# Channel shuffle in place: tiles of 23 KB a partition in place of 24 KB, and a 6 KB tile last

## The chip, the cores and the metric

One core of one Trainium2 chip. Times are device microseconds of one execution; medians of several executions are given. "Span" is the length of the profiled execution as the trace has it, about 1.8 us less than the time of the same execution. A "packet" is what the DMA records list: one row, that is the bytes of one partition of a tile, carried by one of the 16 DMA engines.

## The reference

```python
batch, h, w, c = 16, 64, 64, 256          # float32, groups = 8
x = x.reshape(batch, h, w, groups, c // groups)
x = x.transpose(0, 1, 2, 4, 3)            # channel g*32+j goes to j*8+g
x = x.reshape(batch, h, w, c)
```

67.1 MB come in and 67.1 MB go out; each pixel's 256 floats (1 KB) are permuted in the same way. There is no arithmetic.

## The kernel before

The pixels are cut into tiles of 128 partitions with q pixels (q KB) a partition. A tile is loaded by one DMA on the load queue (issued by SyncE), permuted in pieces of 8 KB a partition by VectorE into PSUM (a second on-chip memory), copied back in place by ScalarE, and stored by one DMA on the store queue (issued by ScalarE). In HBM a partition's q KB are contiguous, and the next partition's follow at once, so "KB between rows" is q as well.

```python
_SIZES = [24] * 20 + [8, 24]
_BUFS = 8
_PIECE = 8
...
    for q in _SIZES:
        buf = pool.tile([P, biggest * c], F32, name="buf")
        nc.sync.dma_start(out=buf[:, : q * c], in_=rows(x_flat, first, q))
        for k in range(0, q, _PIECE):
            piece = buf[:, k * c : (k + _PIECE) * c]
            bounce = psum.tile([P, _PIECE * c], F32, name="bounce")     # two of these
            nc.vector.tensor_copy(out=bounce..., in_=piece...)          # "p (i g j) -> p i j g"
            nc.scalar.copy(out=piece, in_=bounce)
        nc.scalar.dma_start(out=rows(out_flat, first, q), in_=buf[:, : q * c])
        first += P * q
```

## Time and profile before

| | before |
|---|---|
| time, median of the 3 runs that the prediction had | 317.83 us (317.72 to 317.91) |
| span | 315.9 us |
| VectorE, ScalarE busy | 227.9 us, 120.3 us |
| load queue, store queue, share of 16 engines | 49.9%, 49.4% |
| HBM traffic | 134.2 MB, 425 GB/s over the span |

How to read it: the two queue shares are time that packets took, as a share of 16 DMA engines' span, so their sum tells how full the DMA engines are. VectorE at 72% and DMA at 99.3% are averages; which of them sets the end has to be read from stretches and waits.

### The profile page before, as it was taken

The numbers are of one execution on the slowest core, as the hardware profiler recorded it, in microseconds if no ns is written. First come the engines' busy times: TensorE is split into PE (matmuls) and PEld (weight loads), VectorE is DVE, ScalarE is ACT, GpSimd is POOL, SyncE is SP. The second block draws the span as 40 slices with busy tenths as digits, with TensorE's granted clock in tenths as the row PEclk, the third lists the DMA queues.
The fourth block names the chain that finished last, engine by engine and source line by source line (L and its number), as shares of the span: only waits on it lengthen the run. The fifth ranks groups of instructions, "written<-read, shape, count | busy, mean of one in ns | idle before, by whom it ended". The sixth has DMA issues, their size and how long they took to land.

```text
span 315.9 us, 289 instructions
## 1 busy us (share of the span) xinstructions
DVE 227.9 (72%) x64; ACT 120.3 (38%) x65; POOL 0.2 (0%) x4
## 2 busy tenths in 40 slices
DVE  0699999959587685957008986999970299999900
ACT  0354455525252424330015416545500444555420
POOL 0000000000000000000000000000000000000000
DMA  8999999999999999999999999999999999999997
GB/s 296 439 442 380 436 429 433 433 439 433 423 442 433 426 442 426 426 442 426 433 436 427 433 436 436 433 426 437 433 423 448 423 429 444 429 423 433 439 432 302
DMA packets 6338, 134.24 MB, mean 425 GB/s; under 512 B 704, under 2 KB 704, under 8 KB 704
## 3 DMA queue, kind: packets, MB, share of 16 engines
q1 hardware_dynamic: 3168, 67.11, 49.9%
q10 hardware_dynamic: 3168, 67.11, 49.4%
q14 instruction: 2, 0.02, 0.0%
HBM read 67.11 MB, written 67.11 MB: 425 GB/s over the span
## 4 chain that ended last, share of the span: by engine, by line
DVE 54%; another core or an unknown queue 23%; issue 8%; ACT 5%; DMA 3%; DVEq 1%; ACTq 0%
DVE bounce L54 54%; ACT buf L58 5%; DMA buf<-in_x_dram 3%; DVEq L91 1%; ACTq L59 0%; DVEq L54 0%; ACTq L58 0%
## 5 line engine op out<-in xcount | busy, mean ns | idle before, releaser
L54 DVE COPY bounce<-buf 128x2048 f32<-128x2048 f32 x64 | 227.9, 3636 | 72.6 <-ACT buf L58 38.8
L58 ACT COPY buf<-bounce 128x2048 f32<-128x2048 f32 x64 | 119.0, 1866 | 171.1 <-DVE bounce L54 115.3
L58 ACT ACT_TABLE_LOAD x1 | 1.3, 1283 | 11.1 <-DMA buf<-in_x_dram 11.1
L77 POOL MEMSET const-bfloat16-1.0<- 128x1 bf16 x1 | 0.1, 102 | 0.0
L77 POOL MEMSET const-uint8-127<- 128x1 uint8 x1 | 0.1, 101 | 0.0
L77 POOL MEMSET const-float32-0.0<- 128x1 f32 x1 | 0.1, 99 | 0.2 <-issue 0.2
L77 POOL MEMSET const-float32-1.0<- 128x1 f32 x1 | 0.1, 98 | 0.0
## 6 DMA issues: line engine op xcount, KB each, us to landing
buf<-in_x_dram SPq DMA_DIRECT2D x21, 3072.0 KB, 58.4
out_dram<-buf ACTq DMA_DIRECT2D x21, 3072.0 KB, 24.2
buf<-in_x_dram SPq DMA_DIRECT2D x1, 1024.0 KB, 46.0
out_dram<-buf ACTq DMA_DIRECT2D x1, 1024.0 KB, 15.8
```

What stands on the lines that cost most here:

```text
L54: nc.vector.tensor_copy(out=bounce.rearrange("p (i j g) -> p i j g", j=CPG, g=G), in_=piece.rearrange("p (i g j) -> p i j g", g=G, j=CPG),)
L58: nc.scalar.copy(out=piece, in_=bounce)
L77: nc = _bacc.Bacc("TRN2", target_bir_lowering=False, num_devices=1)
L91: with _tile.TileContext(nc) as tc:
```

## The change

Its intent, by its title: rows an odd number of KB apart (kinder to memory), and a small tile last (a shorter tail). Everything else is meant to stay, the eight buffers too.

```diff
-_SIZES = [24] * 20 + [8, 24]
+_SIZES = [23] * 22 + [6]
 _BUFS = 8
+_STORE = 23
 _PIECE = 8
...
-        for k in range(0, q, _PIECE):
-            piece = buf[:, k * c : (k + _PIECE) * c]
...
-        nc.scalar.dma_start(out=rows(out_flat, first, q), in_=buf[:, : q * c])
+        for a in range(0, q, _STORE):
+            b = min(a + _STORE, q)
+            for k in range(a, b, _PIECE):
+                piece = buf[:, k * c : min(k + _PIECE, b) * c]
...                                      # the same two copies, on 8, 8 and 7 KB
+            cols = slice(a * c, b * c)
+            nc.scalar.dma_start(out=rows(out_flat, first, q)[:, cols], in_=buf[:, cols])
```

More of the change, by code (lines that the diff above doesn't have):

```diff
@@ L26 @@
     nc = tc.nc
-    b, h, w, c = x.shape
+    n, h, w, c = x.shape
     G = int(groups)
@@ L30 @@
     assert G * CPG == c
-    assert sum(_SIZES) * P == b * h * w
+    assert sum(_SIZES) * P == n * h * w
     biggest = max(_SIZES)
@@ L50 @@
         nc.sync.dma_start(out=buf[:, : q * c], in_=rows(x_flat, first, q))
-        for k in range(0, q, _PIECE):
-            piece = buf[:, k * c : (k + _PIECE) * c]
-            bounce = psum.tile([P, _PIECE * c], F32, name="bounce")
-            nc.vector.tensor_copy(
-                out=bounce.rearrange("p (i j g) -> p i j g", j=CPG, g=G),
-                in_=piece.rearrange("p (i g j) -> p i j g", g=G, j=CPG),
-            )
-            nc.scalar.copy(out=piece, in_=bounce)
-        nc.scalar.dma_start(out=rows(out_flat, first, q), in_=buf[:, : q * c])
+        for a in range(0, q, _STORE):
+            b = min(a + _STORE, q)
+            for k in range(a, b, _PIECE):
+                piece = buf[:, k * c : min(k + _PIECE, b) * c]
+                bounce = psum.tile([P, _PIECE * c], F32, name="bounce")
+                nc.vector.tensor_copy(
+                    out=bounce[:, : piece.shape[1]].rearrange("p (i j g) -> p i j g", j=CPG, g=G),
+                    in_=piece.rearrange("p (i g j) -> p i j g", g=G, j=CPG),
+                )
+                nc.scalar.copy(out=piece, in_=bounce[:, : piece.shape[1]])
+            cols = slice(a * c, b * c)
+            nc.scalar.dma_start(
+                out=rows(out_flat, first, q)[:, cols], in_=buf[:, cols]
+            )
         first += P * q
```

## The prediction

> **What bounds the kernel now.** I read the page's first two sections first, to see which resource is full, then the DMA queues, then a table of stretches to see where it is not full, then the waits, to see whether the compute engines have room, and last the packet records behind the DMA rows. Busy shares and slices of the page:
>
> ```profile
> span 315.9 us, 289 instructions
> DVE 227.9 (72%) x64; ACT 120.3 (38%) x65; POOL 0.2 (0%) x4
> ...
> DVE  0699999959587685957008986999970299999900
> ...
> DMA  8999999999999999999999999999999999999997
> ...
> q1 hardware_dynamic: 3168, 67.11, 49.9%
> q10 hardware_dynamic: 3168, 67.11, 49.4%
> ```
>
> The reader is to see that VectorE has holes in the middle (whole slices at 0), ScalarE is at 38%, and the DMA row is at 9 in every slice but the first and the last. The load queue (q1) and the store queue (q10) together fill 49.9 + 49.4 = 99.3% of 16 engines' span. The kernel moves 67.11 MB in and 67.11 MB out, so this is a copy with a shuffle hidden inside it. How well is it hidden, and where is the rate lost? The table of stretches (columns: stretch, its length, busy time of each engine with counts, clock, DMA share, GB/s):
>
> ```profile
> 0.00:8.00 8.00, 0.00 (x0) 0.00 (x0) 0.20 (x4) 1.00 0.82 301
> 8.00:24.00 16.00, 12.95 (x4) 6.88 (x4) 0.00 (x0) 1.00 1.01 433
> 24.00:32.00 8.00, 8.00 (x3) 3.73 (x2) 0.00 (x0) 1.00 1.02 399
> 32.00:160.00 128.00, 92.99 (x27) 46.63 (x25) 0.00 (x0) 1.00 1.00 432
> 160.00:286.00 126.00, 99.42 (x28) 53.70 (x29) 0.00 (x0) 1.00 1.01 432
> ...
> 314.00:316.00 2.00, 0.00 (x0) 0.00 (x0) 0.00 (x0) 1.00 0.00 0
> ```
>
> From 8 us to the last 2 us the rate is 432 to 433 GB/s, except for one dent from 24 to 32 us, where the first stores begin beside the loads. The dent costs 8 x (1 - 399/433) = 0.6 us, and the start 8 x (1 - 301/433) = 2.4 us. The waits:
>
> ```profile
> DVE bounce L54 <- ACT buf L58: 38.8, 4, 18.8
> DVE bounce L54 <- DMA buf<-in_x_dram: 33.9, 7, 11.1
> SPq L50 <- DMA out_dram<-buf: 209.9, 14, 22.0
> ```
>
> VectorE waits for data and for ScalarE (which in turn stood 55.7 us waiting for loads), and the load queue's issuer waits 209.9 us for stores to free a buffer. None of these waits costs time, because the table shows the DMA engines full meanwhile: while a load is held back, stores run, and the other way round. So the end is set by bytes over 16 DMA engines. The page's chain of waits, 54% VectorE and 23% unknown queue, is not the bound: it follows one sequence of releases, and the DMA is full under all of it.
>
> The packet records say the same to the nanosecond. A 24576-byte row takes 912 ns in both queues from the 10th to the 90th percentile, and the 8192-byte rows of the one small tile take 309 ns, all 256 of them. Hence (912 - 309) / 16384 = 0.0368 ns a byte (27.2 GB/s an engine) plus 309 - 8192 x 0.0368 = 7.5 ns a row. Each engine moves 8 rows of each tile in each direction.
>
> **What the Trainium skill says.** "DMA: Bandwidth & Descriptors", section "Where 436 GB/s comes from", puts a ceiling of 435.2 GB/s on 16 engines and their ports, shared by all that the core moves. The trace agrees: 16 x 27.2 GB/s is 435, and 432 to 433 with the 7.5 ns a row. The kernel is at that ceiling. Its section "Why small descriptors are slow" has a fixed cost for each packet of about 3 cycles; the trace has 7.5 ns a row, larger, but under 1% of a 24 KB row. Its section "Latency and other measured facts" has HBM row pitches at large powers of two slowing copies (512 KiB and up), cured by a pad of 4 KiB. That is the only ground I find for wanting an odd number of KB between rows. The trace speaks against it here: the pitch is 24 KB, not of that kind, and the rows already move at the ceiling rate. "SBUF — State Buffer", section "SBUF: two separate sides", says that engine accesses and DMA do not contend; in this trace the DMA rate is 432 to 433 GB/s while VectorE is busy and 428 or more when it is not, so different compute piece sizes should not touch it.
>
> **The change part by part.**
>
> The tiles: 22 of 23 KB a partition and one of 6 KB, in place of 21 of 24 KB and one of 8 KB (second to last). Bytes are equal: 22 x 23 + 6 = 21 x 24 + 8 = 512 KB a partition. Row times by the line above: 23552 bytes: 7.5 + 866.8 = 874.3 ns; 6144 bytes: 7.5 + 226.1 = 233.6 ns.
> - Before, each engine: 21 x 8 x 2 = 336 rows x 912 ns = 306.43 us, and 16 x 309 ns = 4.94 us, together 311.38 us, with 44 completion packets of 9 ns (0.40 us) 311.78 us.
> - After, each engine: 22 x 8 x 2 = 352 rows x 874.3 ns = 307.75 us, and 16 x 233.6 ns = 3.74 us, together 311.49 us, with 46 completion packets (0.41 us) 311.90 us.
> - Difference: +0.12 us, on the path.
>
> The copies: each 23 KB tile is worked as 8 + 8 + 7 KB, so there are 22 x 3 + 1 = 67 pieces in place of 64. The order of VectorE and ScalarE is otherwise unchanged; the loop over stores has one round, as 23 is the whole tile. In an unbroken stretch successive ScalarE copies start 3.55 us apart (14.69, 18.24, 21.79 us), that is 0.444 us for each KB, so a 23 KB tile takes about 10.2 us of VectorE. Its two transfers take 2 x 8 x 874.3 ns = 14.0 us. VectorE keeps 27% of room, and the three extra pieces are hidden.
>
> The buffers: still eight, of 23 KB, so 184 KB in flight in place of 192. The store that frees a buffer comes a little earlier for each tile. This only rearranges the waits that cost nothing.
>
> The start: the first store was issued at 23.7 us. With a first load shorter by 128 KB (0.3 us at 433 GB/s) and a last piece shorter by 1 KB (0.44 us) it comes at about 22.9 us. The engines are full of loads then, so nothing is won. The first data moves at 1.74 us in either case.
>
> The end: in before the last data packet ends at 314.56 us and the span 1.3 us later. The last load had landed by 285.7 us; from there on there were (314.56 - 285.7) x 433 GB/s = 12.5 MB of stores to move, four tiles, about two of them already queued. The last store was issued at 302.5 us, so 12.1 us of stores lay before the end, of which its own 3.15 MB are 7.3 us: 4.8 us of older stores still stood in the queue. The final tile's compute chain is therefore already hidden, and a smaller last tile wins nothing there. It can't shorten a tail that is full of bytes.
>
> The sum: 317.83 + 0.12 = 317.95 us. I round to 318.0.
>
> **The rivals.**
>
> 1. The odd pitch helps memory. For it: the diff's wording, and the skill's note on pitch. Against it: the rows have no spread to gain; all of the time that load packets took above 912 ns comes to 1.76 us an engine, about 0.95 of it in the first packets (the ramp) and 0.76 in the dent. If the dent went away entirely, the time would be 318.0 - 0.7 = 317.3 us. It can't reach 2%: even with no dent and no ramp, first data at 1.74 us, 311.9 us of packets, 1.3 us of end and the 1.9 us between span (315.9) and measured time (317.8) give 316.8 us.
>
> 2. A smaller last tile shortens the tail. For it: the usual gain of such a tile where the last store is exposed. Against it: the 4.8 us of older stores that stood before it. It would make nothing of the time; at most it lowers the risk of a gap.
>
> 3. The phases shift so that the engines run dry at the end: after the last load lands, VectorE feeds a tile only each 10.2 us, while a store drains one in 7.0 us; with few stores queued at that moment the queue would empty. For it: the load and store queues swing (VectorE has slices of 0 and slices of 9), and which of the two is long when the loads end is a matter of phase. Against it: stores lag loads from the first 22 us on, in which only loads run (about 9 MB, three tiles), and the lag shrinks only while no load is queued. With 9 MB (21 us) of stores open and at most two tiles (23 + 6 KB, 13 us of VectorE and 2 of ScalarE) uncomputed, there is no gap. If it happened, 1 to 4 us: 319 to 322 us.
>
> 4. A 23 KB row costs more than the line says (some size that is not a multiple of 8 KB split badly by the engine). The trace before has only two sizes, so the line is untested between them. 2% would need 18 ns more a row; both sizes divide by 256 bytes, and I see no reason.
>
> **Range and chances.** The arithmetic leaves +0.1 us; rivals 1 and 2 could take 0.7 to 1.2 us off, rivals 3 and 4 could add 1 to 4. Executions of one kernel agree within about 0.1 us here (317.72 to 317.91). So 318.0 us, with 316.8 to 319.4 for 8 times in 10. Faster by over 2% means under 311.5 us, less than the packets alone take: 1%. Slower by over 2% means over 324.2 us, which needs a gap longer than any I can construct: 2%. Within 2%: 97%.
>
> **What would show it.** Right: packets of about 874 ns for the 23 KB rows in both queues and 234 ns for the 6 KB rows; a DMA row at 9 in all slices but the ends; 432 to 433 GB/s from 32 us to near the end; a span of about 316.0 us; VectorE's busy time within 2% of 227.9 us in 67 pieces, and its holes moved but harmless. Rival 1 would show no dent around 24 to 32 us. Rival 3 would show slices under 9 near the end and VectorE busy up to the last few us. Rival 4 would show packets over 880 ns. The prediction is wrong if the middle stretches hold anything but 432 to 433 GB/s, or if the DMA stands idle between the first load and the last store.

## The result, and the profile after

The changed kernel takes 317.60 us (median of 4, 317.42 to 317.69) beside 317.77 us for the kernel before (317.69 to 317.91, now with a fourth run). The ratio is 0.9993, 95% interval 0.9976 to 1.0011: the same. (A ratio is the mean time of one kernel's fast runs over that of the other's of the same rounds, so it is not quite the ratio of the medians.)

Page of the changed kernel: busy shares, slices and queues.

```profile
span 315.8 us, 300 instructions
DVE 228.1 (72%) x67; ACT 120.9 (38%) x68; POOL 0.2 (0%) x4
...
DMA  8999999999999999999999999999999999999997
...
q1 hardware_dynamic: 3312, 67.11, 49.9%
q10 hardware_dynamic: 3312, 67.11, 49.4%
```

The DMA row and the two shares are those of before to the last digit, with 3312 packets a queue in place of 3168. Its table of stretches, cut at the same times as before (stretch, length, busy time of the engines with counts, clock, DMA share, GB/s):

```profile
8.00:24.00 16.00, 13.11 (x4) 6.67 (x4) 0.00 (x0) 1.00 1.00 430
24.00:32.00 8.00, 8.00 (x4) 4.32 (x3) 0.00 (x0) 1.00 0.99 383
32.00:160.00 128.00, 98.74 (x29) 49.53 (x28) 0.00 (x0) 1.00 1.00 433
160.00:286.00 126.00, 93.09 (x28) 50.89 (x29) 0.00 (x0) 1.00 1.00 432
286.00:303.00 17.00, 15.15 (x5) 9.50 (x6) 0.00 (x0) 1.00 1.00 432
```

The long stretches stay at 432 to 433 GB/s, and the dent at 24 to 32 us is still there (383 GB/s, 399 before; by the packet records the long load packets cost each engine 0.78 us, 0.76 before). The waits moved by a few us and still cost nothing:

```profile
DVE bounce L58 <- DMA buf<-in_x_dram: 36.5, 8, 10.9
DVE bounce L58 <- ACT buf L62: 36.4, 2, 18.5
SPq L52 <- DMA out_dram<-buf: 215.2, 15, 21.8
```

In the packet records the 23 KB rows take 874 ns in both queues from the 10th to the 90th percentile, and the 6 KB rows 234 ns. From the first data packet to the end of the last one it is 312.79 us, and 312.82 us before.

### The profile page after: what moved, and what is told of

It is laid out like the page before. It is cut to its first block, busy times and chain, and to the rows that moved or that the text cites. A ratio compares the mean times of both kernels' runs of the same rounds, so it can differ in the third digit from the quotient of the medians.

```text
span 315.8 us, 300 instructions
## 1 busy us (share of the span) xinstructions
DVE 228.1 (72%) x67; ACT 120.9 (38%) x68; POOL 0.2 (0%) x4
## 3 DMA queue, kind: packets, MB, share of 16 engines
q1 hardware_dynamic: 3312, 67.11, 49.9%
q10 hardware_dynamic: 3312, 67.11, 49.4%
## 4 chain that ended last, share of the span: by engine, by line
DVE 47%; DMA 25%; another core or an unknown queue 16%; issue 4%; ACT 3%; DVEq 1%; ACTq 0%; SPq 0%
DVE bounce L58 47%; DMA buf<-in_x_dram 19%; DMA out_dram<-buf 7%; ACT buf L62 3%; DVEq L98 1%; ACTq L64 0%; DVEq L58 0%; ACTq L62 0%; SPq L52 0%
## 5 line engine op out<-in xcount | busy, mean ns | idle before, releaser
L58 DVE COPY bounce<-buf 128x2048 f32<-128x2048 f32 (+2 forms) x67 | 228.1, 3481 | 73.1 <-DMA buf<-in_x_dram 36.5
L62 ACT COPY buf<-bounce 128x2048 f32<-128x2048 f32 (+2 forms) x67 | 119.6, 1790 | 170.8 <-DVE bounce L58 120.0
## 6 DMA issues: line engine op xcount, KB each, us to landing
out_dram<-buf ACTq DMA_DIRECT2D x1, 768.0 KB, 12.2
```

What stands on the lines that cost most here:

```text
L58: nc.vector.tensor_copy(out=bounce[:, : piece.shape[1]].rearrange("p (i j g) -> p i j g", j=CPG, g=G), in_=piece.rearrange("p (i g j) -> p ...
L62: nc.scalar.copy(out=piece, in_=bounce[:, : piece.shape[1]])
```

## The experiments

All are edits of the changed kernel, which was 317.60 us; each was timed against the kernel before on its own chip (median 317.57 to 317.62 us in all three sets), so a difference to 317.6 us can be read directly.

### 1. No compute at all

```diff
-            for k in range(a, b, _PIECE):
-                ... both copies ...
```

> The changed kernel with the VectorE and ScalarE copies taken out: every tile is loaded and stored unshuffled (a wrong result on purpose). If 16 DMA engines' bytes set the end, as I hold: 317.6 us as for the changed kernel, within 316.5 to 319 (the last store can't start before the last load has landed, which may now leave a small gap at the end), and packets of 874 ns as before. Rival, that part of the compute chain (47% VectorE in the page's chain) lies on the path: at least 6 us less, under 311.6 us. Rival, that compute slows the DMA: packets under 874 ns.

Measured: 317.19 us (317.14 to 317.51), ratio to before 0.9986 (0.9971 to 1.0001). The result is wrong: loads and stores alone. Page and stretches of this kernel (its table has a column for GpSimd only):

```profile
span 315.4 us, 124 instructions
...
8.00:16.00 8.00, 0.00 (x0) 1.00 1.00 389
32.00:160.00 128.00, 0.00 (x0) 1.00 1.00 432
```

What follows: taking away 228 us of VectorE and 120 us of ScalarE work wins at most some 0.4 us, inside the interval of "the same". The compute chain, 47% of the page's chain of the changed kernel, is not on the path, and the packets are 874 ns with or without it, so compute doesn't slow the DMA. The dent came earlier, with the earlier stores (the 8 to 16 us stretch, 389 GB/s).

### 2. An even pitch: 22 KB

```diff
-_SIZES = [23] * 22 + [6]
+_SIZES = [22] * 23 + [6]        # and _STORE = 22
```

> The changed kernel with 23 tiles of 22 KB and the 6 KB tile: an even number of KB between rows. The row model (7.5 ns + 0.0368 ns a byte) gives 22528-byte packets of 836.6 ns and 312.05 us of packets an engine against 311.90: 317.75 us. Rival, that an odd pitch is better for memory: packets longer than 837 ns and more than 318.5 us.

Measured: 317.63 us (317.50 to 317.95), ratio 0.9996 (0.9980 to 1.0013); packets of 836 ns. What follows: odd or even makes no difference that runs with a scatter of 0.2% can show.

### 3. A power-of-two pitch: 16 KB

```diff
-_SIZES = [23] * 22 + [6]
+_SIZES = [16] * 32              # _STORE = 16
-_BUFS = 8
+_BUFS = 11
```

> 32 tiles of 16 KB, a power of two between rows[...], with 11 buffers so that 176 KB stay in flight. The row model gives 16384-byte packets of 610.5 ns, 512 rows and 64 completions an engine: 313.16 us of packets against 311.90, so 318.9 us. Rival, that power-of-two pitch hurts: packets well over 611 ns, 321 us or more.

Measured: 319.21 us (319.16 to 319.41), ratio 1.0049 (1.0034 to 1.0064); packets of 611 ns in both queues from the 10th to the 90th percentile. What follows: the kernel loses 1.6 us, where the row count alone was to cost 1.3, and the packets have the length that their bytes give. So for 16 to 24 KB no effect of the distance between rows is seen beyond the number of rows. In all these runs the rows lie one right after the other, so their distance is always their length; rows with a gap between them were not tried.

### 4. The small tile first

```diff
-_SIZES = [23] * 22 + [6]
+_SIZES = [6] + [23] * 22
```

> The 6 KB tile first in place of last, the same rows otherwise. My theory: the end is full of queued stores, so a full-sized last tile costs nothing: 317.6 us, within 0.5 us. The first store then comes at about 10 us in place of 22.9, and the dent in the rate that stood at 24 to 32 us should move to about 10 to 14 us with it if it belongs to the first stores, and stay at 24 to 32 if it belongs to the loads. Rival, that the small last tile saved part of the tail: about 2 to 5 us more, 320 to 323 us.

Measured: 317.87 us (317.73 to 318.29), ratio 1.0008 (0.9993 to 1.0023). Its stretches near the start:

```profile
8.00:16.00 8.00, 3.71 (x2) 1.50 (x2) 0.00 (x0) 1.00 0.99 401
16.00:24.00 8.00, 8.00 (x3) 5.05 (x3) 0.00 (x0) 1.00 1.02 430
24.00:32.00 8.00, 8.00 (x3) 3.98 (x3) 0.00 (x0) 1.00 1.01 397
```

What follows: a full-sized last tile costs some 0.3 us by the medians and 0.15 us by the data stretch (312.94 us against 312.79), so the small tile saved no tail of 2 to 5 us. On the dent neither reading was right: there are now two. By the packet records the load packets that start from 10 to 14 us take longer, after the first store was issued at 9.4 us (the place that the first reading gave), a few more from 17 to 20 us, and again those from 26.3 to 27.9 us. That second group follows the issue of the first 23 KB store (24.3 us); the store queue, empty since 22.3 us, has its next packet at 28.2 us.

### 5. Stores in three pieces, as each is ready

```diff
-_STORE = 23
+_STORE = 8
```

> The changed kernel with each 23 KB tile stored in three pieces of 8, 8 and 7 KB, each as soon as it is ready. Row model: 2 more store rows for each of 176 rows an engine, 352 x 7.5 ns = 2.64 us, and 44 more completions of 9 ns = 0.40 us: 317.6 + 3.0 = 320.6 us, store packets of 309 and 271 ns. Rival, that the cost of a row is hidden by the other queue on the engine: 317.6 us. Rival, that earlier stores help: under 317 us.

Measured: 334.73 us (334.49 to 335.07), ratio 1.0537 (1.0522 to 1.0553). A miss: three of the 17 us were expected. The store packets have the expected length (309 and 272 ns). The waits and the last stretches:

```profile
ACT buf L62 <- DMA out_dram<-buf: 107.7, 24, 9.2
DVE bounce L58 <- ACT buf L62: 87.9, 20, 12.3
...
280.00:300.00 20.00, 20.00 (x7) 10.77 (x6) 0.00 (x0) 1.00 0.83 345
300.00:332.00 32.00, 27.11 (x9) 15.72 (x9) 0.00 (x0) 1.00 0.75 308
```

The first line is new: ScalarE waits 107.7 us for stores, and then VectorE waits 87.9 us for ScalarE, for there are only two PSUM buffers between them. In the compiled program the reason can be read: the DMAs of both queues take turns on eight completion semaphores (numbers 99, 100 and 103 to 108; a completion semaphore is the counter that tells that a DMA has finished), so a store's issue waits for an earlier DMA to have finished, and as ScalarE issues the stores, its copies stand behind that wait. With four DMAs a tile in place of two the wait comes round sooner. The same wait stands in both main kernels, where it costs nothing: in the changed one the issue of a store (L64) stood 24.6, 3.2 and 21.5 us before such a semaphore, which is nearly all of the 50.7 us that its page has as ScalarE waiting for loads. VectorE falls behind while the DMA is still full (429 GB/s from 32 to 160 us), by the end all eight buffers hold loaded data, and after the last load has landed (278.7 us) there are 47 us of VectorE work with nothing else to move. From 280 us on 20 x 345 + 32 x 308 = 16.8 MB take 52 us where 433 GB/s would take 39: 13 us are lost there. Together with the 3 us of rows that is 16 of the measured 17. A second cause was possible: from 36 to 82 us, with work in both queues nearly throughout, the stores moved 5.1 MB and the loads 14.7 MB (some 110 and 320 GB/s), so stores may simply have been starved. Runs 9 and 10 were made to part the two.

### 6. Rows of 48 KB

```diff
-_SIZES = [23] * 22 + [6]
+_SIZES = [48] * 10 + [32]       # _STORE = 48
-_BUFS = 8
+_BUFS = 4
```

> Ten tiles of 48 KB and one of 32 KB, four buffers (192 KB), the same 8 KB pieces. Row model: 49152-byte packets of 1816.5 ns and 32768-byte packets of 1213.5 ns, 310.26 us of packets an engine against 311.90: 1.6 us less, 316.0 us, if the queues do not run dry. With four buffers of double size the first store comes at about 37 us and the last store is of 32 KB; if the engines run dry at the end, the gain goes and it is 317 to 325 us, with a stretch near the end under 430 GB/s.

Measured: 318.28 us (317.66 to 318.83), ratio 1.0015 (0.9995 to 1.0034). The packets are 1815 and 1213 ns, so the rows did get cheaper by 1.6 us. The records show where it went back: when the last packet ends, the engines no longer finish together (in the last 2.6 us of data they are busy 29% of the time, about 1.9 us lost against 0.4 in the changed kernel), and the dent cost 1.25 us in place of 0.8. That is most of the 2.3 us by which the time misses the 316.0 us of the row model. No stretch before the end was short of data: 433 GB/s from 280 to 300 us.

### 7 and 8. Three buffers, two buffers

```diff
-_BUFS = 8
+_BUFS = 3        # run 7;  2 in run 8
```

> The changed kernel with three buffers in place of eight. A tile alone needs 7.0 us of load, 10.2 us of VectorE and 1.7 of ScalarE, 7.0 us of store and about 2 us for each landing, some 30 us (an estimate from the durations of the profile); three buffers give a tile every 10 us at best against 14.0 us of DMA. My theory: mostly hidden still, with gaps: 318 to 328 us. Rival, that eight buffers are needed: over 330 us.

> The changed kernel with two buffers. By the same sum a tile comes every 15 us or more, above the 14.0 us of DMA, so here the compute chain must show: 340 to 380 us, the DMA row under 9 through the middle. If it still were 318 us, the DMA bound as I read it would be wrong in what keeps the queues full.

Measured: three buffers 334.47 us (333.57 to 334.87), ratio 1.0524 (1.0506 to 1.0543), outside what the theory gave and in the range of its rival (over 330 us; run 12 shows that four buffers already suffice for all but 1%); two buffers 406.07 us (405.01 to 406.40), ratio 1.2777, some 26 us above the 340 to 380 us that were expected. First a stretch of the run with three buffers, then the queues of the run with two:

```profile
32.00:160.00 128.00, 90.18 (x27) 47.52 (x27) 0.00 (x0) 1.00 0.99 409
```

```profile
q1 hardware_dynamic: 3312, 67.11, 45.6%
q10 hardware_dynamic: 3312, 67.11, 38.7%
```

With three buffers the engines are 99% busy and yet move 409 GB/s. The packets are longer: 919 ns in the mean for loads and 896 for stores against 874, which is 176 x (45 + 22) ns = 12 us an engine. The long ones come in groups, most often around the moment when a queue that had run empty starts again, and they are mostly packets of the other queue; most such groups cost each engine 0.7 to 0.9 us, some 0.2 to 0.4. The changed kernel has 1.7 us of such time an engine, so some 10 of the 17 us are long packets; the other 7 are idle engines (the queues' shares add up to 97.2% of 333.1 us in place of 99.3% of 315.8). With two buffers both happen, long packets (1033 ns in the mean for loads) and idle engines (45.6 + 38.7 = 84.3%). The sum behind both expectations was too small: with two buffers a load took 11.4 us to land and a store 12.0 us (medians of the page), where it had some 9 each; with the compute that is 35 us for a tile, or 17.7 us a tile with two buffers, and not 15. So the slack of eight buffers is real, and what too few buffers cost is long packets around restarts and idle engines.

### 9. Stores cut by partitions

```diff
-            nc.scalar.dma_start(out=rows(...)[:, cols], in_=buf[:, cols])
+            for p0, p1 in ((0, 48), (48, 96), (96, 128)):
+                nc.scalar.dma_start(out=rows(...)[p0:p1, cols], in_=buf[p0:p1, cols])
```

> The changed kernel with each tile's store cut by partitions into three (48, 48 and 32 partitions, whole 23 KB rows), issued together when the tile is done: as many stores and as many waits of a store's issue for earlier completions as in the run with stores of 8 KB, but store packets as long as load packets. If that run lost its time because an engine alternates packets of the two queues, so that short store packets got a quarter of the rate and loads ran ahead: about 318 us here (0.4 us for 44 more completions). Rival, that the number of stores in flight and the waits of their issue did it: 325 us or more here too.

Measured: 382.41 us (378.15 to 383.89; the slowest of the four counts as slow), ratio of the fast runs 1.1996 (1.1925 to 1.2067). This run does not decide the question, because it brought in a third thing. Its store packets take 1160 ns in the mean, and one in a hundred over 3393 ns, and where only stores run the rate is about half:

```profile
316.00:380.00 64.00, 36.71 (x11) 22.08 (x13) 0.00 (x0) 1.00 0.85 227
```

The Trainium skill's "SBUF — State Buffer", section "Door 1: The DMA port swizzle", says that partitions 0 to 63 reach only 8 of 16 ports, some 218 GB/s, and 64 to 127 the other 8. The first and the last of the three stores lie in one half each; the measured 227 GB/s, at 85% of the engines' time, is of that size. That the ports are the cause was not tried by itself.

### 10. Loads and stores both in pieces of 8 KB

```diff
-_STORE = 23
+_STORE = 8
-        nc.sync.dma_start(out=buf[:, : q * c], in_=rows(x_flat, first, q))
+        for a in range(0, q, _STORE):
+            cols = slice(a * c, min(a + _STORE, q) * c)
+            nc.sync.dma_start(out=buf[:, cols], in_=rows(x_flat, first, q)[:, cols])
```

> Loads and stores both cut into pieces of 8, 8 and 7 KB: packets of equal length in both queues again, still more completions to wait for. Row model: 704 more rows of 7.5 ns an engine are 5.3 us, 88 more completions 0.8 us: 323.7 us if unequal packet length was what cost the run with short stores its time. Rival, the waits of issues for earlier completions (there are now six DMAs a tile in place of two or four): 330 us or more.

Measured: 330.22 us (329.90 to 330.63), ratio 1.0394. The rows cost what they should (427 GB/s from 32 to 160 us where 433 were), but the lag at the end stays:

```profile
ACT buf L64 <- DMA buf<-in_x_dram: 85.2, 8, 21.7
DVE bounce L60 <- ACT buf L64: 80.7, 17, 20.0
...
300.00:316.00 16.00, 16.00 (x6) 8.90 (x5) 0.00 (x0) 1.00 0.73 300
```

What follows: with packets of equal length in both queues VectorE still waits 80.7 us for ScalarE and ScalarE for DMAs, and at the end VectorE runs without a pause while the DMA stands at 73%. Of the 12.6 us that this run takes more than the changed kernel, rows and completions were to cost 6.1; some 6.5 are lost at the end. Unequal packets are thus not needed for a loss. The trace puts ScalarE's 85.2 us directly before the issue of stores (L66), eight waits that each end with a completion semaphore, so the waits of issues for earlier completions are the likeliest cause. That is read from the trace and not shown by a run of its own: a run with run 5's stores issued by an engine without copies would try it, and was not made. How the 13 us of run 5 divide between waits and unequal packets is not settled either.

### 11. An attempt at less time: 32 KB rows, small tiles last

```diff
-_SIZES = [23] * 22 + [6]
+_SIZES = [32] * 15 + [26, 6]    # _STORE = 32
-_BUFS = 8
+_BUFS = 6
```

> An attempt at less time: 15 tiles of 32 KB, one of 26 and one of 6 KB, six buffers (192 KB). Row model: 240 rows of 1213.5 ns, 16 of 987.4 and 16 of 233.6, 310.78 us of packets an engine and 34 completions, against 311.49 and 46: 0.8 us less, so 316.8 us. Rival, that longer packets leave the engines unequal at the end, as in the run with 48 KB rows: 317.5 us or more.

Measured: 319.19, 324.57, 322.74 and 331.07 us; ratio of the fast runs 1.0106 (1.0041 to 1.0171). Not faster, and unsteady as no other kernel here: two of the four count as slow. The profile fell in the quickest run (span 317.4 us): packets of 1213, 987 and 234 ns, as the row model has them, 430 to 432 GB/s through the middle. Even there the end loses about 2.1 us an engine (busy 19% of the last 2.6 us of data), as in run 6 and as the expectation's rival had it. Why the other runs took longer can't be read from it and stays open.

### 12. Four buffers

```diff
-_BUFS = 8
+_BUFS = 4
```

> The changed kernel with four buffers. Three buffers gave 334 us, with a queue that kept running empty and packets that took longer after each restart (2% to 5% in the mean). If that is the cause, four buffers should leave few restarts: 318 to 323 us, load packets with a mean under 890 ns against 919 with three. If all eight buffers are needed, 325 us or more.

Measured: 320.33 us (319.93 to 320.67), ratio 1.0085 (1.0070 to 1.0100); load packets 884 ns in the mean.

```profile
32.00:160.00 128.00, 95.68 (x29) 49.81 (x29) 0.00 (x0) 1.00 1.00 433
160.00:280.00 120.00, 87.98 (x26) 47.60 (x27) 0.00 (x0) 1.00 1.01 433
300.00:316.00 16.00, 7.91 (x3) 5.40 (x4) 0.00 (x0) 1.00 0.83 352
```

What follows: four buffers keep the middle full. What they lack is the store of work at the end: the last load lands at 302.4 us in place of 287.4, and the last tiles' compute then lies open (352 GB/s from 300 to 316 us). The store queue then stands empty from 305.8 to 307.8 us, 2.0 of the 2.7 us. This is the gap of the prediction's third rival, made to happen.

No version beat both kernels by more than the scatter.

## Why the prediction was right

The time (317.6 us) lies in the range, 0.4 us from the point, and "the same" had 97%. By its steps:

- **The bound.** It held that DMA bytes set the end and that no wait costs time. Run 1 shows it: without compute 317.19 us. Some of its readings on the way were too smooth. "From 8 us to the last 2 us the rate is 432 to 433 GB/s, except for one dent" left out two lines of the same answer:

```profile
286.00:303.00 17.00, 14.53 (x5) 9.32 (x5) 0.00 (x0) 1.00 0.99 428
303.00:314.00 11.00, 0.00 (x0) 0.00 (x0) 0.00 (x0) 1.00 0.98 419
```

Nor is the rate "432 to 433 GB/s while VectorE is busy and 428 or more when it is not": 399 stands beside a full VectorE (24 to 32 us) and 419 beside an idle one. That compute does not touch the DMA rests on run 1, with 432 GB/s and 874 ns packets and no compute at all. And 24576 bytes in 912 ns on 16 engines are 431 GB/s, where it wrote 432 to 433. None of this moves its result.
- **The row times.** 874.3 and 233.6 ns were worked out from two sizes; 874 and 234 ns were measured. Runs 2, 3, 5, 6 and 11 add six sizes (table below), all within 1.5 ns. This was the term with the best ground under it.
- **The sum.** +0.12 us was predicted; the medians differ by -0.17 us, and the data stretch by -0.03 us (312.79 against 312.82). Both are below the scatter of the runs, so the sign of so small a term was neither shown nor refuted. "The same" is earned by the bound, not by this term. (The 1.9 us between span and time, in rival 1, came from two different executions; within one it is 1.8 us.)
- **The compute.** 67 pieces with 228.1 us of VectorE; the first store at 22.9 us, as worked out. The 7 KB piece takes 3213 ns, seven eighths of the 8 KB piece (3631 ns) being 3177: a fixed part of small size, hidden.
- **Rival 1, the pitch.** Refuted as predicted: the dent stayed, and 16, 22 and 23 KB behave as the row model says (the result and runs 2 and 3).
- **Rival 2, the tail.** Refuted as predicted (run 4). In the changed kernel the last store was issued at 302.65 us and took 12.2 us to land, of which its own 0.79 MB are 1.8 us: some 10 us of older stores stood before it.
- **Rival 3, the dry end.** It didn't happen with eight buffers (432 GB/s from 286 to 303 us). Run 12 shows that with four it does, in a run that took 2.7 us more, and runs 5 and 10 that it comes with eight too, there with compute held back, by the trace at the issue of stores. The prediction argued it away from the bytes in flight alone; it did not consider that the store's issuer is also a compute engine, though the 55.7 us that it read as ScalarE waiting for loads were nearly all waits of a store's issue (25.5, 3.1, 6.6 and 18.7 us). That was harmless here, because the change keeps one store a tile.
- **Rival 4, a dear row.** Refuted: 874 ns.

## What to carry to other kernels

When the DMA engines' shares add up to 99% and the long stretches show the ceiling rate, what a change of tile size can win in the middle is the number of rows, and a row's fixed cost tells its worth before anything is run: time two packet sizes in the trace and draw the line. Longer rows can lose it again at the end (runs 6 and 11). Be wary of splitting a tile's store where a compute engine issues the stores: here it cost 5%, though the DMA was the bound. In the trace the issuing engine waits for earlier completions and takes the compute with it; how much of the loss is due to that was not tried by itself. The pages' chain of waits can be half compute in a kernel in which compute costs nothing; a run without compute settles it.

## What the Trainium skill lacked or had wrong

- "DMA: Bandwidth & Descriptors", "Why small descriptors are slow": a fixed cost of about 3 cycles a packet (3.5 ns if they are cycles of the page's 850 MHz fabric, an estimate). Here a row costs 7.5 ns + 0.0368 ns a byte, in both directions:

| bytes of a row | 6144 | 7168 | 16384 | 22528 | 23552 | 26624 | 32768 | 49152 |
|---|---|---|---|---|---|---|---|---|
| line from 8192 and 24576 bytes, ns | 233.6 | 271.3 | 610.5 | 836.6 | 874.3 | 987.4 | 1213.5 | 1816.5 |
| measured, ns | 234 | 272 | 611 | 836 | 874 | 987 | 1213 | 1815 |

- The same page, "Latency and other measured facts", has HBM row pitches at large powers of two (512 KiB and up) slow, and contiguous tiles as one cure. It does not say whether the length of such contiguous rows matters: at 16, 22, 23 and 24 KB, a power of two or not, they showed no effect beyond the row count.
- The same page, "Queues, rings and completion order", has an engine alternate between queues by packet. It does not draw the consequence for packets of unequal length: 23 KB load rows beside 7 to 8 KB store rows got some 320 and 110 GB/s (run 5, 36 to 82 us), about 3 to 1, which is what turns of one packet each would give.
- No page that I read has the cost of a queue that starts again after running empty: groups of longer packets, mostly of the other queue, 0.7 to 0.9 us an engine for most groups; once in the kernel before (0.76 us, at the first store), and 12 us of longer packets in all with three buffers. In the changed kernel the first store is issued at 22.9 us, the long load packets start from 25.1 us on, and the first store packet at 26.5 us. The mechanism is not shown here, and not every restart has it: in the changed kernel the store queue runs empty at 166.2 us and starts again at 175.3 us, with no packet there over 888 ns.
- No page that I read has what it costs when a store's issue waits on a completion semaphore that the compiled program shares among DMAs, and so holds back the compute of the engine that issues it: 107.7 us of ScalarE in run 5.
